# Stick-breaking attention: the softplus of the next step issued before the sum of the present one, half of its roundings on ScalarE

## The chip, the cores and the metric

The kernel runs on one core of one Trainium2 chip. The metric is the device time of one execution in microseconds, here the median of three runs. Engines are named TensorE (PE in the profile), VectorE (DVE), ScalarE (ACT), GpSimd (POOL) and SyncE (SP).

## What is computed

One layer of a decoder trunk: a modulated norm and input projection, a gated MLP beside stick-breaking attention, an output projection, then a mixture of 32 experts. The change touches the attention alone. With `z = q k / sqrt(128)` for 1024 tokens and 4 heads, it is

```python
log_fail = jnp.where(causal, jax.nn.log_sigmoid(-z), 0.0)
within = jnp.einsum('bhqni,ij->bhqnj', log_fail, after_in_block)
later = lax.cumsum(blk, axis=3, reverse=True) - blk
log_a = jax.nn.log_sigmoid(z) + (within + later[..., None])
a = jnp.where(causal, jnp.exp(log_a), 0.0)
outs.append(jnp.einsum('bhqk,bhkd->bhqd', a.astype(vt.dtype), vt[:, :, :kl]))
```

Here `-log_sigmoid(-z)` is the softplus of `z`, and `blk` is the sum of `log_fail` over a block of 128 keys.

## The kernel before, in words

The attention works on transposed scores: 128 keys on the partitions, up to 512 queries (half of the sequence) along the columns. A `Chain` is one head and one half of the queries; it goes through its blocks of keys `j` from the last to the first, 4 blocks in the first half and 8 in the second. A block on the diagonal needs only part of the columns: widths are 128, 256, 384, 512 in the first half and 128, 256, 384, then five times 512 in the second. Two chains (two heads, of even and odd number) run together as a pair; `seq` lists the 24 steps, each a block of both chains, twelve of them 512 wide and four of each other width.

In a step, for each chain: `z` (L655, with the mask L659 on the diagonal) makes the scores on TensorE; `e0`, `e1`, `e2` (L664, L669, L673) make log(1 + exp(-|z|)) on ScalarE; `sp` (L681) on VectorE makes the softplus max(z, 0) + e, `sh` (L682) rounds it to the matrix format, `sl` (L683) on GpSimd takes the remainder, so that the products with triangles of ones keep the precision; `ls` (L689) makes log_sigmoid(z); `tri` (L697 for `sh`, L698 for `sl`) adds the sum inside the block to `cum` in PSUM; `add` (L702) adds `cum` to `ls`; `comp` (L708, L709) completes `cum` to the sum over the whole block for the later steps, after `add` has read it; `exp` (L713) and the product with the values `av` (L719) finish it.

The order on every engine is written out by hand (`manual_schedule`): each engine's queue holds its instructions in the order of the program. In round `k` of the loop this is: tri(k), add(k), z(k+2), comp(k), av(k-1), sp(k+1) with its sh and sl, ls(k+1), e0(k+2), exp(k), e1(k+2), e2(k+2). When a pair is finished, six closing parts are put at the end of the next rounds: fin0 copies and squares the output (ScalarE, L724, L726), fin1 sums the squares on TensorE (L730) and takes a power on GpSimd (L128), fin2 spreads it by 16 products (L736), fin3 scales (VectorE, L740), fin4 rounds (ScalarE, L744), fin5 takes the remainder (VectorE, L748). The fourth pair is closed in the output projection that follows (L867).

Buffers that matter: four `z` in PSUM (two steps), two `sp`, four each of `e`, `sh` and `sl`, eight `ls`, two `cum`.

Of the kernel before, what the change touches and what calls it, by code (L numbers as in the profile page):

```python
# [13 lines left out]
AF = mybir.ActivationFunctionType  # L14
# [44 lines left out]
def body(ctx, tc, A, out):  # L59
    nc = tc.nc  # L60
    V, G, T, SC, SY = nc.vector, nc.gpsimd, nc.tensor, nc.scalar, nc.sync
# [364 lines left out]
    def at(s, fn):  # L426
        todo.setdefault(s, []).append(fn)
# [192 lines left out]
    def wo_load(i):  # L620
        if i < 16:
            cg, b = i // 4, (i + 2) % 4
            wo_raw[i] = wr.tile([P, 2, 512], F32, name="wo")
            SY.dma_start(wo_raw[i], A["w_out"][cg, b])
# [8 lines left out]
    def ya_load(t):  # L633
        y = op.tile([P, DG], F32, name="yld")
        SY.dma_start(y, y_d[t * P:(t + 1) * P, :])
        return y

    with ExitStack() as c3:
# [4 lines left out]
        class Chain:  # L643
# [31 lines left out]
            def sp(self, j):  # L675
                z, e = self.k[j]
                q0 = self.q0(j)
                sp = at_.tile([P, 512], F32, name="sp", bufs=2)[:, q0:]
                sh = at_.tile([P, 512], F32R, name="sh")[:, q0:]
                sl = at_.tile([P, 512], F32R, name="sl")[:, q0:]  # L680
                V.scalar_tensor_tensor(sp, z, 0.0, e, op0=ALU.max, op1=ALU.add)  # L681
                V.tensor_copy(sh, sp)  # L682
                G.tensor_tensor(sl, sp, sh.bitcast(F32), op=ALU.subtract)  # L683
                self.k[j] += [sh, sl]

# [66 lines left out]
        with tc.manual_schedule():  # L752
            seq = []
            for half in range(2):
                for hp2 in range(2):
                    ch = [Chain(half, 2 * hp2), Chain(half, 2 * hp2 + 1)]
                    seq += [(ch, j) for j in range((half + 1) * HT - 1, -1, -1)]
            n = len(seq)

            def each(i, f):  # L760
                if 0 <= i < n:
                    ch, j = seq[i]
                    for c in ch:
                        f(c, j)

            for i in range(2):
                wo_load(i)
            G.dma_start(wgr, A["w_gr"])
            yas = {t: ya_load(t) for t in range(2)}

            def scores(i):
                for f in (Chain.e0, Chain.e1, Chain.e2):
                    each(i, f)

            def first(i):
                return 0 <= i < n and seq[i][1] == seq[i][0][0].top

            each(0, Chain.z)
            each(1, Chain.z)
            scores(0)  # L780
            each(0, Chain.sp)
            each(0, Chain.ls)
            scores(1)
            for k in range(n + 1):
                each(k, Chain.tri)
                each(k, Chain.add)
                each(k + 2, Chain.z)
                each(k, Chain.comp)
                if 0 < k and seq[k - 1][1] == 0:
                    for i in range(6):  # L790
                        for c in seq[k - 1][0]:
                            at(k + (0, 1, 1, 1, 2, 3)[i], getattr(c, f"fin{i}"))
                if first(k - 2):
                    each(k - 2, Chain.av)
                if not first(k - 1):
                    each(k - 1, Chain.av)
                each(k + 1, Chain.sp)
                each(k + 1, Chain.ls)
                each(k + 2, Chain.e0)
                each(k, Chain.exp)  # L800
                each(k + 2, Chain.e1)
                each(k + 2, Chain.e2)
                for f in todo.pop(k, []) if k < n else ():
                    f()
            fins = [f for k in sorted(todo) for f in todo[k]]
            todo.clear()
# [710 lines left out]
```

## Time and profile before

| | us |
|---|---|
| median of 3 runs | 1617.72 (1617.65 to 1617.85) |
| profiled run, its own time | 1615.23 |
| its span, first to last instruction | 1613.4 |
| attention stage in the span | 535 to 663 |

The profile is of one execution. A row of the timeline gives the start in us from the start of the span, the duration, the engine, the source line, the operation with output and inputs, and in brackets how long the engine had been idle and who ended it. Instructions of one kind in a row are merged (x2: two, with one duration for both). The name `ls` stands for the tile that `ls`, `add` and `exp` share, `e` for that of `e0`, `e1`, `e2`. PEclk is the granted clock of TensorE, 1.00 for the upper of its two levels. The stage was cut out by the first `z` and the last `sl`.

### The profile page before, as it was taken

The page shows a single profiled execution, that of the slowest core. Times are in us where ns is not written, and L with a number is a line of the kernel's source. Part 1 is how long each engine was busy: PE and PEld are TensorE (multiplying, and loading weights), DVE is VectorE, ACT ScalarE, POOL GpSimd, SP SyncE. Part 2 cuts the span into 40 slices and gives each one's busy share as a digit, 9 for nine tenths or more (in the row PEclk, how much of TensorE's full clock was granted, in tenths as well). Part 3 has the DMA queues.
Part 4 walks back from the last instruction along what each step waited for, and adds up shares of the span by engine and source line. Part 5 has one row for each costly group of instructions (what it writes and reads, how often), then busy time and mean ns, then how long its engine had stood idle before and what let it go on. Part 6 is the DMA issues. An engine that isn't in the chain of part 4 may idle for free.

```text
span 1613.4 us, 21346 instructions
## 1 busy us (share of the span) xinstructions
PE 1518.8 (94%) x6818; PEld 1151.6 (71%) x6818; DVE 1221.2 (76%) x2220; ACT 945.1 (59%) x2014; POOL 315.2 (20%) x288
## 2 busy tenths in 40 slices
PE   4999998999999899899999869999989999999996
PEld 4788887888888665578878656666656666666664
DVE  5889675867787588668856768887868888888883
ACT  5442588755434667432223467777767777777771
POOL 2000132010011334320001322324221212211111
PEclk8899999999999999999999979999989999999998
DMA  9987478768776000468857568999999999999972
GB/s 378 351 315 242 155 260 297 258 238 310 279 258 228 1 1 1 154 211 299 291 187 289 200 209 318 354 369 346 387 341 365 360 361 370 366 362 356 358 299 33
DMA packets 94394, 433.94 MB, mean 269 GB/s; under 512 B 13073, under 2 KB 13185, under 8 KB 64193
## 3 DMA queue, kind: packets, MB, share of 16 engines
q1 hardware_dynamic: 82000, 377.54, 63.3%
q0 software_dynamic: 11984, 52.85, 11.2%
q10 hardware_dynamic: 288, 2.10, 0.3%
q8 instruction: 56, 0.92, 0.2%
q14 instruction: 66, 0.53, 0.1%
HBM read 399.89 MB, written 43.02 MB: 275 GB/s over the span
## 4 chain that ended last, share of the span: by engine, by line
PE 40%; DMA 34%; issue 13%; DVE 5%; ACT 4%; POOL 2%; POOLq 0%; another core or an unknown queue 0%; SPq 0%; DVEq 0%; ACTq 0%
DMA out<-y,idx 22%; PE acc L322 22%; PE acc L867 9%; DMA xg<-u_d,idx 7%; DMA out<-xi 2%; DMA wm<-in_w_mod 2%; PE lg L913 1%; PE yp L719 1%; POOL sl L683 1%; PE z L655 1%; DVE macc L182 1%; DVE sp L681 1%; ACT junk L347 1%; DVE sh L682 1%; PE tr L906 1%
## 5 line engine op out<-in xcount | busy, mean ns | idle before, releaser
L1282 DVE TENSOR_TENSOR wl<-wx,wh 128x1024 fp32r<-128x1024 f32 x256 | 309.5, 1219 | 13.5 <-ACT wh L1281 12.5
L1281 ACT ACTIVATE wh<-wx 128x1024 fp32r<-128x1024 f32 x256 | 273.4, 1070 | 49.0 <-PE gu L1291 34.8
L1314 PE MATMUL dn<-wx,actT 128*128 128x512 f32 x512 | 242.4, 597 | 6.1 <-DMA wx<-in_w_down 5.5
L1291 PE MATMUL gu<-wh,xh 128*128 128x512 f32 x512 | 239.7, 468 | 0.0
L182 DVE SCALAR_TENSOR_TENSOR macc<-wm,sc_c,macc 128x512 f32<-128x512 f32 x296 | 222.2, 751 | 11.5 <-DMA wm<-in_w_mod 3.4
L322 PE MATMUL acc<-wh,hh 128*128 128x512 f32 x640 | 209.8, 398 | 3.4 <-ACT hh L278 1.8
L322 PE MATMUL acc<-wl,hh 128*128 128x512 f32 x640 | 206.7, 393 | 2.9 <-DVE wl L307 2.7
L322 PE MATMUL acc<-wh,hl 128*128 128x512 f32 x640 | 206.6, 393 | 0.4 <-DVE hl L279 0.4
L1291 PE MATMUL gu<-wl,xh 128*128 128x512 f32 x512 | 203.1, 397 | 0.1
L1291 PE MATMUL gu<-wh,xl 128*128 128x512 f32 x512 | 201.9, 394 | 0.0
L1224 POOL DMA_INDIRECT out<-y,idx x52 | 94.9, 1825 | 459.2 <-DVE y L1315 453.1
L1315 DVE TENSOR_TENSOR y<-dn,gate 128x512 f32<-128x512 f32 x128 | 88.5, 692 | 112.0 <-PE dn L1314 101.6
L867 PE MATMUL acc<-wo,yh 128*128 128x512 f32 x512 | 169.3, 412 | 0.0
L1270 ACT ACTIVATE xh<-tp,b2c 128x128 fp32r<-128x128 f32 x512 | 146.8, 383 | 17.8 <-PE tp L1265 17.7
L1314 PEld LDWEIGHTS dn<-wx,actT 128*128 128x128 f32 x512 | 96.5, 189 | 82.6 <-issue 63.1
L1272 DVE SCALAR_TENSOR_TENSOR xl<-tp,b2c,xh 128x128 fp32r<-128x128 f32 x512 | 143.5, 343 | 3.9 <-ACT xh L1270 3.9
L322 PEld LDWEIGHTS acc<-wl,hh 128*128 128x128 f32 x640 | 120.7, 189 | 30.0 <-DVE wl L307 5.0
L322 PEld LDWEIGHTS acc<-wh,hl 128*128 128x128 f32 x640 | 121.2, 189 | 26.9 <-DVE hl L279 1.1
L322 PEld LDWEIGHTS acc<-wh,hh 128*128 128x128 f32 x640 | 119.6, 190 | 27.6 <-ACT hh L278 1.9
L307 DVE TENSOR_TENSOR wl<-w,wh 128x1024 fp32r<-128x1024 f32 x80 | 97.6, 1221 | 34.2 <-ACT wh L306 34.1
L306 ACT ACTIVATE wh<-w 128x1024 fp32r<-128x1024 f32 x80 | 83.0, 1053 | 63.1 <-PE acc L322 51.6
L1291 PEld LDWEIGHTS gu<-wl,xh 128*128 128x128 f32 x512 | 97.4, 190 | 30.2 <-issue 15.1
(246 smaller groups left out, 2326.7 us busy)
## 6 DMA issues: line engine op xcount, KB each, us to landing
wx<-in_w_gu SPq DMA_DIRECT2D x128, 1024.0 KB
wm<-in_w_mod SPq DMA_DIRECT2D x160, 512.0 KB
wx<-in_w_down SPq DMA_DIRECT2D x64, 1024.0 KB
w<-in_w_in SPq DMA_DIRECT2D x80, 512.0 KB
x<-in_w_mod SPq DMA_DIRECT2D x16, 1024.0 KB
wo<-in_w_out SPq DMA_DIRECT2D x16, 512.0 KB
xi<-in_x SPq DMA_DIRECT2D x24, 256.0 KB
out<-xi SPq DMA_DIRECT2D x24, 256.0 KB
```

The costliest lines, as they stand in the source:

```text
L182: V.scalar_tensor_tensor(self.acc, t[:, j, :], sc, self.acc, op0=ALU.mult, op1=ALU.add)
L307: V.tensor_tensor(wl, w, wh.bitcast(F32), op=ALU.subtract)
L322: T.matmul(accs[t], a, b, start=(first and j == 0 and n == 0), stop=(last and j == 1 and n == 2))
L867: T.matmul(acc, y[a][:, c, ts_], w[b][:, c % 2, :], start=(n_ == 0 and i == 0), stop=(n_ == 7 and i == 2))
L1224: return G.indirect_dma_start(out=out, out_offset=bass.IndirectOffsetOnAxis(ap=idx, axis=0), in_=y, in_offset=None, bounds_check=S - 1, oo ...
L1270: SC.activation(xh[:, j, :], self.p[:, j, :], AF.Identity, bias=b2c[:, b * 4 + j:b * 4 + j + 1])
L1272: V.scalar_tensor_tensor(xl[:, j, :], self.p[:, j, :], b2c[:, b * 4 + j:b * 4 + j + 1], xh[:, j, :].bitcast(F32), op0=ALU.add, op1=ALU.sub ...
L1281: SC.activation(self.wh[q], w, AF.Copy)
L1282: low = lambda: V.tensor_tensor(self.wl[q], w, self.wh[q].bitcast(F32), op=ALU.subtract)
L1291: T.matmul(self.gu, a[c // 4][:, c % 4, :], b[q][:, k, :], start=(c == 0 and i == 0), stop=(c == 15 and i == 2))
L1314: T.matmul(d, self.aT[:, f, :], self.wd[f][:, cs], start=(f == 0), stop=(f == 1))
L1315: V.tensor_tensor(self.y[:, cs], d, gate2[:, cs], op=ALU.mult)
```

## The change

It does two things. `sp` of the next step, with its rounding `sh` and its remainder `sl`, is issued right after the triangular product of the present step and ahead of `add`, where it stood behind `av`. And the rounding of every chain with an odd head number is done by ScalarE instead of VectorE. As the calls are ordered, that instruction stands in ScalarE's queue ahead of `e0`. Nothing else moves.

```diff
@@ -679,7 +679,10 @@
                 V.scalar_tensor_tensor(sp, z, 0.0, e, op0=ALU.max, op1=ALU.add)
-                V.tensor_copy(sh, sp)
+                if self.h % 2:
+                    SC.activation(sh, sp, AF.Copy)
+                else:
+                    V.tensor_copy(sh, sp)
                 G.tensor_tensor(sl, sp, sh.bitcast(F32), op=ALU.subtract)
                 self.k[j] += [sh, sl]
@@ -783,6 +786,7 @@
             for k in range(n + 1):
                 each(k, Chain.tri)
+                each(k + 1, Chain.sp)
                 each(k, Chain.add)
                 each(k + 2, Chain.z)
                 each(k, Chain.comp)
@@ -794,7 +798,6 @@
                 if not first(k - 1):
                     each(k - 1, Chain.av)
-                each(k + 1, Chain.sp)
                 each(k + 1, Chain.ls)
                 each(k + 2, Chain.e0)
                 each(k, Chain.exp)
```

## Rows read from the trace of the kernel before

**Rows 1.** Busy time by stretch (time, then engines with counts, PEclk, DMA share, GB/s)

```profile
535.00:663.00 128.00, 114.34 (x488) 77.55 (x488) 106.92 (x208) 91.52 (x210) 54.79 (x57) 0.97 0.05 17
586.30:589.80 3.50, 3.48 (x17) 3.48 (x18) 0.75 (x1) 0.85 (x2) 0.95 (x1) 0.56 0.02 5
```

**Rows 2.** Timeline of one wide step (start us, duration us, engine, line, what)

```profile
606.67 1.28 POOL L683 TENSOR_TENSOR sl<-sp,sh 128x512 fp32r<-128x512 f32 x1 [0.45 <-DVE sh L682]
...
608.54 0.69 DVE L702 TENSOR_TENSOR ls<-ls,cum 128x512 f32<-128x512 f32 x1 [0.24 <-PE cum L698]
...
609.14 0.68 DVE L681 SCALAR_TENSOR_TENSOR sp<-z,e 128x512 f32<-128x512 f32 x1
...
609.86 0.43 DVE L682 CAST sh<-sp 128x512 fp32r<-128x512 f32 x1
...
610.21 0.68 DVE L681 SCALAR_TENSOR_TENSOR sp<-z,e 128x512 f32<-128x512 f32 x1
...
610.92 1.11 DVE L682 CAST sh<-sp 128x512 fp32r<-128x512 f32 x1
...
611.79 1.14 ACT L669 ACTIVATE e<-e 128x512 f32<-128x512 f32 x2
...
612.20 1.29 POOL L683 TENSOR_TENSOR sl<-sp,sh 128x512 fp32r<-128x512 f32 x1 [0.45 <-DVE sh L682]
...
612.83 1.14 ACT L673 ACTIVATE e<-e 128x512 f32<-128x512 f32 x2
```

**Rows 3.** Groups by line, 535 to 665 us (busy, mean ns, then idle before)

```profile
L664 ACT ACTIVATE e<-z 128x512 f32<-128x512 f32 (+3 forms) x48 | 22.9, 489 | 32.8 <-PE z L659 16.5 <-PE z L655 16.2
```

**Rows 4.** The largest product group of the output projection, from the page

```profile
L867 PE MATMUL acc<-wo,yh 128*128 128x512 f32 x512 | 169.3, 412 | 0.0
```

**Rows 5.** Timeline of a step 256 columns wide

```profile
555.70 0.71 ACT L673 ACTIVATE e<-e 128x256 f32<-128x256 f32 x2
...
556.20 0.42 DVE L681 SCALAR_TENSOR_TENSOR sp<-z,e 128x256 f32<-128x256 f32 x1 [0.28 <-ACT e L673]
...
556.66 0.29 DVE L682 CAST sh<-sp 128x256 fp32r<-128x256 f32 x1
556.87 0.42 DVE L681 SCALAR_TENSOR_TENSOR sp<-z,e 128x256 f32<-128x256 f32 x1
```

**Rows 6.** Timeline at ScalarE's first and last work in the stage

```profile
535.77 0.25 ACT L664 ACTIVATE e<-z 128x128 f32<-128x128 f32 x1
...
663.71 0.67 DVE L702 TENSOR_TENSOR ls<-ls,cum 128x512 f32<-128x512 f32 x1
...
664.41 0.63 ACT L713 ACTIVATE ls<-ls 128x512 f32<-128x512 f32 x1 [3.95 <-DVE ls L702]
...
665.34 0.63 ACT L713 ACTIVATE ls<-ls 128x512 f32<-128x512 f32 x1 [0.30 <-DVE ls L702]
```

**Rows 7.** Timeline where a pair of chains is closed, twice

```profile
586.32 3.45 PE L736 MATMUL yp<-cst,rs 128*128 128x128 f32 x16 [0.91 <-POOL rs L128]
...
629.05 1.07 ACT L664 ACTIVATE e<-z 128x512 f32<-128x512 f32 x2
...
629.95 1.01 POOL L683 TENSOR_TENSOR sl<-sp,sh 128x384 fp32r<-128x384 f32 x1 [0.39 <-DVE sh L682]
...
630.91 1.99 POOL L128 TENSOR_TENSOR rs<-rs,mhalf 128x4 f32<-128x4 f32 x2
...
631.97 2.14 PE L736 MATMUL yp<-cst,rs 128*128 128x128 f32 x16 [0.92 <-POOL rs L128]
...
634.23 0.75 DVE L740 SCALAR_TENSOR_TENSOR u<-u,hcol,yp 128x512 f32<-128x512 f32 x1 [0.31 <-PE yp L736]
```

**Rows 8.** The chain that ended last, in time order (start us, us, what)

```profile
608.50 1.72 PE z L655 x4
610.22 0.23 PE cum L708
...
611.15 1.72 PE yp L719 x4
```

## The prediction

> **What bounds the kernel now.** I went from the stage to the engine and then to one step. The attention stage fills the stretch from 535 to 663 us of the profiled run; in it VectorE is busy for 106.92 of 128 us, TensorE for 114.34, ScalarE for 91.52, GpSimd for 54.79 [rows 1]. None is full, so a ring of waits must set the pace. The timeline of one step, in which both chains work on tiles of 512 columns, shows it [rows 2]. From one `sl` of the second chain (606.67) to the next (612.20) are 5.53 us, and this ring has no hole in it: `sl` on GpSimd and the triangular product behind it, 1.87 until the sum (`add`) of the second chain starts at 608.54; then on VectorE `add` 0.60 to the start of `sp`, 0.72 to `sh`, 0.35 to the second `sp`, 0.71 to the second `sh`, and 1.28 until the next `sl`. The second `sh` takes 1.11 where the first takes 0.43: it runs while GpSimd works on the first chain's `sl`. ScalarE, in the same step, waits: its `e0` lost 32.8 us in the stage to late scores `z` [rows 3], because `z` stands behind the triangular product, and this behind `sl`. After the stage TensorE goes straight into the output projection, whose products hardly wait (0.0 us before the largest group of them) [rows 4]; what the stage gains or loses reaches the end whole.
>
> **The change, part by part.** *The move* puts `sp`, `sh`, `sl` of the next step ahead of the sum of the present one. On VectorE the queue becomes sp, sh (chain 0), sp (chain 1), add, add, ls, ls; on GpSimd only the `sl` move, ahead of nothing but the powers of the closing steps (costed below), and what is moved issues no DMA, on no queue. It opens the ring above: `sp` no longer stands behind `add`, so the triangular product finds its `sl` ready. Its price is that the two sums, and so `exp` (ScalarE) and the complementary product (TensorE), now stand behind two `sp` that wait for `e2` of ScalarE.
>
> *The rounding on ScalarE* takes the 24 `sh` of the odd chains from VectorE, 1.11 us each in a wide step, and puts them on ScalarE **ahead of** `e0` of the step after. That instruction waits for `sp` of its chain, and behind it are queued e0, e0, exp, exp, e1, e1, e2, e2. The `sp` after it waits for that `e2`. So a new ring arises, ScalarE to VectorE and back, once a step.
>
> Its length in a wide step, counted from the start of `e2` of chain 0: two `e2` take 1.14 and stand 0.52 apart, as the start of `e1` (611.79) and of `e2` (612.83), two instructions each, tell: 1.04 for two. So the first ends at 0.62. From the end of an `e2` to `sp` it takes 0.10: 256 columns wide, a pair takes 0.71 and stands 0.31 apart, so the first ends at 556.10 and `sp` starts at 556.20 [rows 5]. Then 0.72 to `sh`, 0.35 to the second `sp`, 0.68 for it, and 0.03 from VectorE to ScalarE (the sum of 663.71 ends at 664.38, its `exp` starts at 664.41 [rows 6]). ScalarE can start `sh` at 2.50; its second `e2` ended at 1.14; it waits 1.36. From there to the next `e2`: `sh` 0.52, two `e0` 0.95 (1.07 for the pair, with an overlap of about 0.1 [rows 7]), exp 1.04, e1 1.04, together 3.55. The ring is **6.05 us against 5.53**.
>
> What is covered in it: the first sum starts at 2.39 and ends at 3.07, its `exp` is due at 3.97, 0.9 later. `sl` of chain 1 runs from about 3.27 to 4.55, and the triangular product comes round after 5.9. TensorE needs 1.72 for the scores, 1.72 for the value products and eight products with the triangles of 0.23, 5.3 of 6.05 us [rows 8]. VectorE needs 0.72 + 0.35 + 0.60 and four times 0.60, about 4.1. If any of this cover is gone, it adds to the 6.05, and never takes from it.
>
> Not every step is wide, so I sum the stage as a ledger of ScalarE, which works strictly in order: work and waits. **Before:** from its first `e0` (535.77) to the end of its last `exp` (665.34 + 0.63) 130.2 us [rows 6]; waits 32.8 [rows 3] and, for the last two `exp`, 3.95 and 0.30 [rows 6]; work 93.1. **After, work:** 24 `sh` more at the spacing of its instructions, 0.52 for 512 columns and 0.31 for 256 [rows 2, 5], by the line through them 0.41 and 0.20 for 384 and 128; of 24 steps twelve are 512 wide and four each of the others, so 12 x 0.52 + 4 x (0.41 + 0.31 + 0.20) = 9.9; minus about 1.0, because a wait exposes some 0.1 us of an instruction's end and there will be some ten waits fewer: 102.0. **After, waits:** before `sh` 1.36 in a wide step; 0.91 with 256 columns (555.70 to 556.20, 0.46, 0.21, 0.42 and 0.03 give 1.62, less the pair of 0.71); by the line 1.13 and 0.68 for 384 and 128. Where closing work of a finished pair stands in ScalarE's queue it fills these waits: fin4 (1.04) in two wide steps and one narrow one, the copy and the square of fin0 in three of 384. That leaves 7 x 1.36 + 2 x 0.32 + 4 x 0.91 + 3 x 0.68 + 1.13 = 17.0. Three wide `sh` come behind the closing of a pair. There VectorE holds `sp` behind fin3 (L740), which needs the powers on GpSimd and the products L736. From the start of the preceding `sh` (384 wide, behind the square): 0.5 for it, 0.17 to `sl` and 0.96 to its successor (629.95 to 630.91), 1.99 for two powers, 1.33 until fin3 of the second chain (634.23, counted from 632.90), 0.67 until the next instruction of VectorE, now `sp`, then 0.72, 0.35, 0.68, 0.03 as above [rows 2, 7]: 7.4. ScalarE has 4.1 of work in that time (0.41, 0.95, 0.62, 1.04, 1.04), so it waits some 3.2, three times, 9.6. Waits for `z` remain where a narrow `sp` lets ScalarE run ahead of TensorE, after the last wide step of each pair; the trace of before can't show them. They lie between nothing and what `e0` loses now per step (32.8 over 24, 1.4), twice over for three such places, 8; I take 4. The last `exp` waits for `sh` 0.62, `sl` 0.17 + 1.28, product and sum about 1.2: 3.3. Together 33.9. **The sum:** 102.0 + 33.9 = 135.9 against 130.2, **5.7 us longer**.
>
> **TensorE's clock** I leave as it is. It fell in the stage: from 586.3 to 589.8 the mean granted clock was 0.56, partly at the lower of its two levels, 1.2 instead of 2.4 GHz [rows 1], after TensorE had waited 0.91 us for the powers [rows 7]. The sixteen products L736 took 3.45 there and 2.14 at 631.97 [rows 7]; I take the difference, 1.3 us, for one fall. That wait stays in the new order; whether it meets a fall more or less often, no row tells: minus 2 to plus 4 for the range.
>
> **The rivals.** *Faster.* The second `sh` leaves the ring in which it took 1.11, and ScalarE's answer comes early enough. Then TensorE's 5.3 bounds a wide step: twelve times 0.22, 2.6 us, and up to as much again in the narrow steps: 3 to 5 less, **1613 to 1615**. It needs ScalarE's wait before `sh` to be under 1.36 - 0.52 = 0.84. For it: VectorE is the busiest engine apart from TensorE [rows 1], and in wide steps alone it loses 12 x 1.11 = 13 us of casts. Against it: each link of the 2.50 has its row, and they are in series. The Trainium skill, "SBUF — State Buffer", section "Who interferes with whom", says that a cast of VectorE in a mode with two ports and a GpSimd instruction exclude each other, the later one waiting for the whole of the first; the trace agrees (1.11 against 0.43), and by that rule alone the change would give back 0.68 for each wide step, 8 us in twelve.
>
> *No change.* The waits for `z` don't appear (4 less), and at the closings TensorE and VectorE come round earlier than I chain them, with some 0.7 less each: 1617 to 1620.
>
> *Slower than I say.* TensorE's idle time in a step grows from 0.2 to 0.7, and the clock falls in three or four more stretches, at 1.3 each: 4 to 5 on top, about **1628**. The Trainium skill, "TensorE: Matmul & The Clock Gate", section "HAM oscillation — how this bites in real kernels", tells of kernels in which waits between bursts of products keep taking the clock down.
>
> *The move does not do what it says*, because the sums hold up `exp` on ScalarE: it decides once they come over 0.9 us later than I have them. It would add to 6.05 and lies in the upper part of the range.
>
> **How the numbers follow.** The profiled run took 1615.23, the median of three runs is 1617.72, 2.5 more; I add 5.7 to the median: **1623.4**. My forecast (1621 to 1626) gets 0.52, slower still 0.15, no change 0.18, faster 0.15. A measurement of this kernel can tell about 0.2% from no change, 3.2 us. So faster 0.15, same 0.18, slower 0.67. The range leaves out most of faster and the far end of slower: 1616.0 to 1629.5.
>
> **What would show it.** Right: wide steps about 6.05 apart; ScalarE waiting some 26 us before `sh`, named after `sp`, and its waits for `z` down from 32.8 to a few us; the remaining casts of VectorE at 0.43; VectorE idle before `sp`, for `e2`; GpSimd hardly waited for by the triangular product. Wrong: wide steps at 5.3 with ScalarE waiting under 0.84 before `sh`; or `exp` waiting for the sums throughout; or a stage of the same length with its loss in the closings only.

## The result, and the profile after

The changed kernel took 1628.22 us (median of 4 runs, 1626.99 to 1631.31) against 1617.78 for the kernel before: 10.4 us longer, a ratio of 1.0068 with a 95% interval of 1.0054 to 1.0082. The direction was right and the time lies inside the range; the forecast of 1623.4 has about half of the loss. Of all single runs of this study one, of the kernel e4 below, took 1734.0 us at a mean granted clock of 0.84 (the others 0.97 to 0.98) and is left out of its ratio.

The profiled run of the changed kernel took 1629.25, 14.0 more than that of before. The loss splits into three stretches, by ScalarE's first `e0` and the end of its last `exp`:

| | before | after | difference |
|---|---|---|---|
| up to the first `e0` of the stage | 535.77 | 537.52 | +1.75 |
| the stage | 130.20 | 141.35 | **+11.15** |
| from its end to the end of the run | 949.3 | 950.4 | +1.1 |

The first row is not the change's: in the profiled runs of all kernels below this start lies anywhere from 533.8 to 539.7. The stage holds the loss. Its two ends are rows of ScalarE's timeline after (start, duration, engine, line, what):

```profile
537.52 0.25 ACT L664 ACTIVATE e<-z 128x128 f32<-128x128 f32 x1
...
677.64 1.23 ACT L716 ACTIVATE ls<-ls 128x512 f32<-128x512 f32 x2 [4.56 <-DVE ls L705]
```

The projection behind it hands the loss on whole, as before (its largest group of products, from the page after, beside [rows 4]):

```profile
L870 PE MATMUL acc<-wo,yh 128*128 128x512 f32 x512 | 170.5, 414 | 0.0
```

The groups by line of the changed kernel, 535 to 677 us (busy, mean ns, then idle before), stand beside [rows 3]. After, `sp` is L681, `sh` is L683 on ScalarE and L685 on VectorE, `sl` L686, the triangular products L700 and L701, `add` L705, the complementary products L711 and L712, `exp` L716, the value products L722, the closing's products with the powers L739. First two groups of the kernel before (535 to 665 us), then those of the change:

```profile
L681 DVE SCALAR_TENSOR_TENSOR sp<-z,e 128x512 f32<-128x512 f32 (+3 forms) x48 | 26.4, 551 | 2.8 <-ACT e L673 2.7
...
L698 PE MATMUL cum<-sl,tri_r 128*128 128x512 f32 (+3 forms) x48 | 19.1, 401 | 10.7 <-POOL sl L683 10.7
```

```profile
L681 DVE SCALAR_TENSOR_TENSOR sp<-z,e 128x512 f32<-128x512 f32 (+3 forms) x48 | 26.6, 554 | 34.4 <-ACT e L673 17.4 <-issue 16.9
...
L664 ACT ACTIVATE e<-z 128x512 f32<-128x512 f32 (+3 forms) x48 | 21.0, 480 | 5.7 <-PE z L659 5.7
...
L701 PE MATMUL cum<-sl,tri_r 128*128 128x512 f32 (+3 forms) x48 | 17.6, 374 | 0.3
L711 PE MATMUL cum<-sh,comp_r 128*128 128x512 f32 (+3 forms) x40 | 17.1, 438 | 17.2 <-DVE ls L705 17.1
...
L685 DVE CAST sh<-sp 128x512 fp32r<-128x512 f32 (+3 forms) x24 | 8.6, 360 | 1.9
```

The wait for `z` has gone from 32.8 to 5.7 us, and TensorE no longer waits for GpSimd ahead of the second triangular product (0.3 us at L701, where it was 10.7 at L698). In their place VectorE stands idle for 34.4 us before `sp` (2.8 before), and TensorE for 17.2 before the complementary product, for the sums (0.2 before). The waits of ScalarE, from the view of waits (engine and line, waited for: total, times, longest), are:

```profile
ACT sh L683 <- DVE sp L681: 30.3, 20, 4.4
ACT e L664 <- PE z L659: 5.7, 7, 3.2
ACT ls L716 <- DVE ls L705: 4.6, 1, 4.6
```

One wide step after, from the timeline, beside [rows 2]:

```profile
614.70 1.14 ACT L673 ACTIVATE e<-e 128x512 f32<-128x512 f32 x2
...
615.43 0.69 DVE L681 SCALAR_TENSOR_TENSOR sp<-z,e 128x512 f32<-128x512 f32 x1 [2.00 <-ACT e L673]
...
616.22 0.43 DVE L685 CAST sh<-sp 128x512 fp32r<-128x512 f32 x1
...
616.56 0.68 DVE L681 SCALAR_TENSOR_TENSOR sp<-z,e 128x512 f32<-128x512 f32 x1
616.82 2.53 POOL L686 TENSOR_TENSOR sl<-sp,sh 128x512 fp32r<-128x512 f32 x2 [3.70 <-DVE sh L685]
617.16 1.27 DVE L705 TENSOR_TENSOR ls<-ls,cum 128x512 f32<-128x512 f32 x2
617.34 0.63 ACT L683 ACTIVATE sh<-sp 128x512 fp32r<-128x512 f32 x1 [1.50 <-DVE sp L681]
617.88 1.07 ACT L664 ACTIVATE e<-z 128x512 f32<-128x512 f32 x2
...
618.83 1.15 ACT L716 ACTIVATE ls<-ls 128x512 f32<-128x512 f32 x2
...
620.91 1.14 ACT L673 ACTIVATE e<-e 128x512 f32<-128x512 f32 x2
```

From one `e2` to the next are 6.21 us, and the path between them is the ring that the prediction wrote down: `e2`, `sp`, cast, `sp`, then `sh` on ScalarE, and from there ScalarE's own queue. ScalarE waits 1.50 before `sh`.

The 5.53 us that the prediction read off one step are what most wide steps took before, but not all. From the first `sp` of a wide step to that of the next wide one there are eight distances in the second half of the queries. Before, five took 5.5 us, two 6.61 and one 6.23, together 47.1; after, six take 6.21 and two 5.92, together 49.1. In a step of 6.61 VectorE takes the remainders of a finished pair (fin5) ahead of the sums:

```profile
601.01 1.49 DVE L748 TENSOR_TENSOR yl<-u,yh 128x512 fp32r<-128x512 f32 x2
```

After, the same two instructions (L751, at 607.13) find VectorE idle, and their step takes 6.21. So these wide steps lose 2.0 us together.

The granted clock of TensorE, by stretches (time, engines, PEclk; beside [rows 1]: the whole stage, then two places where it fell):

```profile
537.50:676.50 139.00, 118.70 (x483) 79.72 (x484) 85.89 (x184) 99.40 (x233) 56.40 (x58) 0.94 0.05 16
...
552.60:559.40 6.80, 5.92 (x17) 5.18 (x18) 3.90 (x9) 2.89 (x10) 3.36 (x4) 0.51 0.00 1
573.00:576.60 3.60, 3.60 (x19) 3.60 (x17) 2.08 (x3) 0.62 (x2) 0.02 (x1) 0.53 0.00 0
```

The stage as a whole was at 0.97 before and is at 0.94 after; 0.51 is almost wholly the lower of the two levels, 1.2 GHz. Before, the clock fell twice in the stage (566.2 to 569.7 and 586.7 to 590.2, 0.51 in both), after, four times (also 641.2 to 644.7 and 671.9 to 675.4). The first fall, 6.8 us long, has no counterpart before. What TensorE did ahead of it, in the timeline:

```profile
549.82 0.30 PE L659 MATMUL z<-negm_r,ident_r 128*128 128x128 f32 x1
...
553.48 0.69 PE L711 MATMUL cum<-sh,comp_r 128*128 128x384 f32 x1 [3.35 <-DVE ls L705]
...
554.93 2.76 PE L722 MATMUL yp<-ls,x 128*128 128x128 f32 x8
```

TensorE sits idle for 3.35 us, because the scores of that step are 128 columns wide and soon done, while the next products wait for sums that now stand behind two `sp` of 512 columns. This is the step in which the two widths part the most. It took 7.37 us.

### The profile page after: what moved, and what is told of

The parts are those of the page before. It is cut to its first block, busy times and chain, and to the rows that moved or that the text cites. A ratio compares the mean times of both kernels' runs of the same rounds, so it can differ in the third digit from the quotient of the medians.

```text
span 1627.3 us, 21294 instructions
## 1 busy us (share of the span) xinstructions
PE 1524.8 (94%) x6818; PEld 1155.6 (71%) x6818; DVE 1199.4 (74%) x2196; ACT 953.8 (59%) x2038; POOL 315.6 (19%) x288
## 4 chain that ended last, share of the span: by engine, by line
DMA 28%; PE 17%; issue 12%; ACT 5%; DVE 3%; POOL 1%; POOLq 0%; another core or an unknown queue 0%; DVEq 0%; ACTq 0%
DMA out<-y,idx 20%; PE acc L870 9%; DMA xg<-u_d,idx 5%; DMA out<-xi 2%; PE gu L1294 2%; PE lg L916 1%; PE dn L1317 1%; DVE sp L681 1%; PE tr L909 1%; ACT e L669 1%; ACT e L664 1%; ACT ls L716 1%; PE yp L739 1%; PE yp L722 0%; PE tp L1268 0%
## 5 line engine op out<-in xcount | busy, mean ns | idle before, releaser
L1284 ACT ACTIVATE wh<-wx 128x1024 fp32r<-128x1024 f32 x256 | 273.8, 1072 | 47.1 <-PE gu L1294 35.6
```

Source lines behind the costliest of these rows:

```text
L1284: SC.activation(self.wh[q], w, AF.Copy)
```

## The experiments

All times are medians of 4 to 10 runs; each ratio is against the kernel before on the same chip, where that took 1617.0 to 1617.6 (single runs 1611 to 1622). "Stage" is the stretch above in the profiled run (130.2 before, 141.35 after). "Wide step" gives the distance that occurs most often, or the range, and in brackets the mean of the eight distances named above (before 5.53, mean 5.89; after 6.21, mean 6.14).

| kernel | us | ratio (95%) | stage | wide step |
|---|---|---|---|---|
| the change, again (e5) | 1627.82 | 1.0078 (1.0060 to 1.0097) | 141.89 | 6.21 (6.14) |
| move alone (e1) | 1634.64 | 1.0119 (1.0095 to 1.0142) | 151.35 | 6.46 (6.35) |
| rounding alone (e2) | 1628.61 | 1.0082 (1.0058 to 1.0105) | 138.60 | 6.14 (6.09) |
| ScalarE's work without the wait (e3) | 1616.10 | 0.9999 (0.9983 to 1.0015) | 129.23 | 5.52 (5.88) |
| change, TensorE filled (e6) | 1626.14 | 1.0064 (1.0047 to 1.0080) | 135.21 | 6.21 (6.14) |
| the same again (e9) | 1623.81 | 1.0048 (1.0031 to 1.0064) | 138.35 | 6.21 (6.14) |
| move, rounding behind `e0` (e7) | 1625.36 | 1.0057 (1.0035 to 1.0079) | 140.43 | 5.3 to 6.3 (5.79) |
| no move, rounding behind `e0` (e8) | 1619.02 | 1.0022 (1.0010 to 1.0034) | 131.96 | 5.1 to 6.4 (5.57) |
| sum, `sp`, sum, `sp` (e4) | 1611.08 | 0.9967 (0.9954 to 0.9981) | 121.63 | 5.35, 4.7 to 6.0 (5.35) |
| `sp`, sum, sum, `sp` (e10) | 1615.04 | 0.9981 (0.9966 to 0.9997) | 127.13 | 4.7 and 6.1 in turn (5.44) |
| e4, value products earlier (e11) | 1608.39 | 0.9939 (0.9914 to 0.9963) | 121.55 | 4.6 to 6.0 (5.31) |

**Each part alone.** The move without the rounding:

```diff
                 each(k, Chain.tri)
+                each(k + 1, Chain.sp)
                 each(k, Chain.add)
...
-                each(k + 1, Chain.sp)
                 each(k + 1, Chain.ls)
```

> The move alone, all roundings on VectorE as before. Ring theory (what sets the pace is the chain of waits through the queue orders): the sums, and with them exp, now stand behind both sp and both casts of the next step, which wait for e2, and the second cast is still stretched beside GpSimd; counted from an e2 of the first chain, exp can start at about 4.2 and the next e2 at about 6.4, so a wide step takes 6.3 to 6.5 us, ScalarE waits for the sums (10 us and more before exp in the stage), and the kernel is 9 to 15 us slower than before, more than the whole change. Rival (the rounding on ScalarE alone costs the time, the move is harmless or opens the old ring): within 2 us of before, or faster.

It took 17 us more than before, beyond what was expected. Groups by line (here `sh` is L682, `add` L702, `exp` L713), and below them one wide step:

```profile
L682 DVE CAST sh<-sp 128x512 fp32r<-128x512 f32 (+3 forms) x48 | 28.3, 590 | 3.9
...
L713 ACT ACTIVATE ls<-ls 128x512 f32<-128x512 f32 (+3 forms) x48 | 23.4, 521 | 19.7 <-DVE ls L702 19.5
```

```profile
616.47 1.27 POOL L683 TENSOR_TENSOR sl<-sp,sh 128x512 fp32r<-128x512 f32 x1 [3.46 <-DVE sh L682]
...
617.01 1.02 DVE L682 CAST sh<-sp 128x512 fp32r<-128x512 f32 x1
...
617.95 1.27 DVE L702 TENSOR_TENSOR ls<-ls,cum 128x512 f32<-128x512 f32 x2
...
618.65 1.23 ACT L713 ACTIVATE ls<-ls 128x512 f32<-128x512 f32 x2 [0.53 <-DVE ls L702]
```

The stretched cast stays (1.02 beside GpSimd's subtract), now ahead of the sums, and `exp` waits for them, 19.7 us in the stage. Here the rival "the move does not do what it says" is the case. TensorE's clock was at its lower level for 27 us of this stage.

The rounding without the move:

```diff
-                V.tensor_copy(sh, sp)
+                if self.h % 2:
+                    SC.activation(sh, sp, AF.Copy)
+                else:
+                    V.tensor_copy(sh, sp)
```

> The rounding of odd chains on ScalarE alone, sp behind the sums as before. Ring theory: the same ring e2 - sp - sh - sp - rounding on ScalarE - e0 - exp - e1 - e2 is there, since the rounding stands ahead of e0; wide steps 6.1 to 6.2 us, ScalarE waiting some 30 us before the rounding, 4 to 9 us slower than before. Rival (the move is what costs, because the sums hold up exp and the complementary products): within 2 us of before.

It took 11 us more than before, again beyond what was expected. From its groups by line:

```profile
L716 ACT ACTIVATE ls<-ls 128x512 f32<-128x512 f32 (+3 forms) x48 | 22.5, 522 | 1.0 <-DVE ls L705 1.0
...
L664 ACT ACTIVATE e<-z 128x512 f32<-128x512 f32 (+3 forms) x48 | 20.6, 478 | 0.5 <-PE z L659 0.5
```

`e0` and `exp` hardly wait any more; what is left of ScalarE's idle time, 36.9 us, stands before `sh`. The ring through ScalarE is 6.14 a wide step with the sums ahead of `sp`, and the three closings take 10.7 each, with the clock low in them. So each part alone costs as much as the change or more, and the two losses do not add: taking the cast off VectorE gives the move back some 7 us of its 17, and beside the rounding on ScalarE the move brings nothing that can be told from noise (ratios 1.0082 without it, 1.0068 and 1.0078 with it).

**Is it ScalarE's extra work, or the wait?** The kernel before, with 24 copies of `e` of the same sizes at the place of the rounding, into a tile that nothing reads; they wait for nothing new:

```diff
                 V.tensor_copy(sh, sp)
+                if self.h % 2:
+                    SC.activation(at_.tile([P, 512], F32R, name="xx", bufs=1)[:, q0:], e, AF.Copy)
```

> Before, with 24 more copies on ScalarE at the place where the change puts the rounding and of the same size, but of a tile that ScalarE made itself and that nobody reads; casts stay on VectorE. Ring theory: no new wait, and ScalarE has 38 us of waits to take it, so 0 to 3 us slower, wide steps 5.5 us. Rival (ScalarE's additional work of 10 to 12 us is what costs): 7 to 11 us slower.

```profile
L664 ACT ACTIVATE e<-z 128x512 f32<-128x512 f32 (+3 forms) x48 | 22.6, 486 | 20.9 <-PE z L659 11.8 <-PE z L655 9.1
...
L684 ACT ACTIVATE xx<-e 128x512 fp32r<-128x512 f32 (+3 forms) x24 | 12.5, 520 | 0.6
```

12.5 us of work more on ScalarE, no time more: the wait for `z` shrinks from 32.8 to 20.9, by the work that fills it. What costs is not the length of the rounding but its waiting for VectorE at the head of ScalarE's queue; e3 leaves out both the wait and the use of the result, and the place in the queue is varied by itself in e7 and e8 below.

**The clock.** To see the change without falls, products whose result is never read fill TensorE's long waits: four calls of 512 columns (eight products in the trace) ahead of the complementary product of the one step above, and one call of 256 columns for each chain in each of the three closings.

```diff
+            def fill(self, n, w, src):
+                for _ in range(n):
+                    T.matmul(self.yp[:, 0:w], ident, src[:, 0:w], start=True, stop=True, skip_group_check=True)
...
+                if k == 2:
+                    for c in seq[0][0]:
+                        c.yp = py.tile([P, 512], F32, name="yp")
+                        c.fill(2, 512, qT[:, c.h, 0:512])
...
+                        if i == 2 and k < n:
+                            for c in seq[k - 1][0]:
+                                at(k + 1, lambda c=c: c.fill(1, 256, c.sq))
```

> The change, with products that do nothing useful where TensorE waits and its clock fell in the first profile: four of 512 columns in the second round (behind its scores, ahead of the complementary products, which wait 3.35 us there for the sum) and one of 256 columns for each chain in three closings, ahead of the products L739. Nobody reads what they write. If the falls of the clock are what my prediction lacked: no fall near the fourth step and at the closings, that step down from 7.4 to about 5, the closings at 8 to 8.5, the stage 3 to 5 us shorter than the change's own. Rival (the waits alone make the time, the clock follows them at no cost): the stage as long as the change's or up to 3 us longer, by the filling products themselves.

> The change as it is, once more, as the yardstick of the next three on the same chip. Ring theory: wide steps 6.2 us, ScalarE waiting 30 us before the rounding, 8 to 13 us slower than before; the falls of TensorE's clock need not lie in the same places as in the first profile.

The granted clock in the stage of the filled kernel, then its waits on ScalarE, then the step that took 7.37 us in the change (its L739 of this form is the filling):

```profile
538.80:674.00 135.20, 119.42 (x509) 77.67 (x510) 87.07 (x186) 100.60 (x236) 56.47 (x58) 1.00 0.05 16
```

```profile
ACT sh L683 <- DVE sp L681: 28.3, 20, 3.3
ACT e L664 <- PE z L659: 3.1, 7, 1.1
ACT ls L716 <- DVE ls L705: 3.1, 1, 3.1
```

```profile
551.22 3.65 PE L739 MATMUL yp<-xk,cst 128*128 128x512 f32 x8
...
554.74 0.44 PE L711 MATMUL cum<-sh,comp_r 128*128 128x384 f32 x1
...
555.65 1.47 PE L722 MATMUL yp<-ls,x 128*128 128x128 f32 x8
```

The clock stayed at 1.00 throughout, the value products took 1.47 instead of 2.76, and the stage took 135.21 us instead of 141.35. The steps that differ are the four where the change had lost its clock: that step 4.75 for 7.37; the first and third closing (from the first `sp` of the 384-wide step to that of the next) 8.09 and 8.05 for 9.00 and 9.24; the last stretch, from the first `sp` of the last step to the end of the last `exp`, 7.96 for 9.46. Together 2.62 + 0.91 + 1.19 + 1.50 = 6.22, against a difference of 6.14; in the second closing, where the change had not lost its clock, the filling costs 0.11, and every other step is the same to 0.01.

The repeat of the change (e5) tells the same, with five falls, in part at other places. The step after the 3.35 us wait came out at 6.02 there, since its fall was half as long:

```profile
549.30:552.80 3.50, 3.02 (x10) 2.93 (x11) 2.81 (x7) 2.62 (x10) 2.21 (x3) 0.51 0.01 2
```

Against the filled kernel e5 loses 1.28 in that step, 1.64 in the like step at the start of the third pair, 1.09 and 1.18 in two closings and 1.50 in the last stretch: 6.69, which is the whole difference of the stages (141.89 and 135.20).

The median fell by only 1.7 us against the change on the same chip. The profiled run of the filled kernel entered its stage at 538.78, 5 us later than that of the repeated change (533.83), which hides its gain in these two runs (1625.09 and 1626.09); for the medians this is not shown. The second trial:

> The change with the filling products of e6 once more, to see whether the stage of 135.2 us and the missing falls of the clock repeat, and where the time goes that the stage won (its start lay 5 us later than in the change's profile). If the falls are the missing term: no fall between 540 and 670 us, stage 135 to 136 us, median 2 to 6 us under the change's 1627.8. Rival (chance of one execution): falls as in the change, stage 140 us or more.

The median was 6.2 us above the kernel before (ratio 1.0048); the profiled stage 138.35, with two falls left, in one closing (9.81) and in the last stretch (9.46). Less what these two took beyond the 8.16 and 7.96 of e6, it is 135.2 again. So the filling takes falls away (none and two in the profiled stages, four and five without it), not every fall in every execution.

**Where the rounding stands in ScalarE's queue.** Rounding behind `e0` instead of ahead of it, with the move and without (the odd chains' `sh` and `sl` leave `Chain.sp` and are issued by a function of their own):

```diff
+            def rnd(self, j):
+                if self.h % 2:
+                    sh, sl = self.k[j][-2:]
+                    SC.activation(sh, self.sp_, AF.Copy)
+                    G.tensor_tensor(sl, self.sp_, sh.bitcast(F32), op=ALU.subtract)
...
                 each(k + 2, Chain.e0)
+                each(k + 1, Chain.rnd)
                 each(k, Chain.exp)
```

> The change, but the rounding on ScalarE stands behind e0 of the step after instead of ahead of it; sp ahead of the sums as in the change. Ring theory: e0 fills most of the wait before the rounding (1.50 down to about 0.5 in a wide step); but sl of chain 1, and the triangular product behind it, come later, and the sums still stand behind sp: wide steps 5.7 to 6.0 us, 1 to 4 us faster than the change. Rival (ScalarE's queue order does not matter, only that VectorE and ScalarE alternate): as the change.

> Only the rounding of odd chains on ScalarE, behind e0 of the step after; sp behind the sums as before. Ring theory: the ring through ScalarE has slack, the cast of 1.11 is gone from VectorE; wide steps 5.3 to 5.5 us, within 2 us of before or up to 4 us faster, and 8 us or more faster than the rounding ahead of e0. Rival (rounding on ScalarE costs by itself): 4 us or more slower than before.

With the move, ScalarE's wait before `sh` falls from 30.3 to 4.9 us, and the wait of `e0` for `z` comes back, 28.4: the ring closes elsewhere, and 8 us of loss stay. Without the move the wide steps are shorter than before (5.57 in the mean for 5.89; most take 5.1 to 5.4, those with fin5 6.3), as was hoped, but the closings take 10.0 to 11.1 where they took 8.4 to 9.7, and the sum is 2 us longer than before. The timeline of such a closing (here `sh` is L692, `sl` L693, the products with the powers L745):

```profile
630.99 1.06 ACT L664 ACTIVATE e<-z 128x512 f32<-128x512 f32 x2
...
631.94 0.52 ACT L692 ACTIVATE sh<-sp 128x384 fp32r<-128x384 f32 x1
...
632.54 1.00 POOL L693 TENSOR_TENSOR sl<-sp,sh 128x384 fp32r<-128x384 f32 x1 [1.35 <-ACT sh L692]
...
633.50 1.98 POOL L128 TENSOR_TENSOR rs<-rs,mhalf 128x4 f32<-128x4 f32 x2
...
634.56 2.77 PE L745 MATMUL yp<-cst,rs 128*128 128x128 f32 x16 [1.87 <-POOL rs L128]
```

The rounding stands on ScalarE behind the closing's own copies and squares and behind `e0`; `sl` on GpSimd comes after it, and the powers after `sl`. Counted from `e0`, the powers start 2.51 us later, where they started 1.86 later before (630.91 less 629.05 in [rows 7]), and TensorE waits 1.87 for them instead of 0.92.

**Orders on VectorE alone.** If two `sp` ahead of two sums hold up the sums, and two sums ahead of two `sp` hold up `sl`, then one of each in turn should do better than both, with every cast on VectorE (`one(k, c, f)` runs `f` for chain c of step k alone; `sp` is gone from its place behind the value products):

```diff
-                each(k, Chain.add)
+                for c in range(2):
+                    one(k, c, Chain.add)
+                    one(k + 1, c, Chain.sp)
```

> No rounding on ScalarE; on VectorE the order is sum of chain 0, sp and cast of chain 0, sum of chain 1, sp and cast of chain 1. Ring theory: between the two casts now lie a sum and an sp (about 1.3 us), so the second cast hardly meets GpSimd's 1.28 us of the first and falls from 1.11 to about 0.5; sp of chain 0 waits for one sum only; a wide step is then bounded by TensorE, 5.3 us against 5.53, and the kernel is 2 to 6 us faster. Rival (VectorE's order does not matter because the clock of TensorE and the closing steps set the stage): within 2 us of before.

It beats the kernel before by 0.33% (1611.08), at the upper end of what was expected, with a stage of 121.63 and no fall of the clock in it. One of its wide steps in the timeline (lines as in the kernel before):

```profile
608.45 0.69 DVE L702 TENSOR_TENSOR ls<-ls,cum 128x512 f32<-128x512 f32 x1 [0.66 <-PE cum L698]
...
609.06 0.68 DVE L681 SCALAR_TENSOR_TENSOR sp<-z,e 128x512 f32<-128x512 f32 x1
...
609.77 0.43 DVE L682 CAST sh<-sp 128x512 fp32r<-128x512 f32 x1
...
610.12 0.68 DVE L702 TENSOR_TENSOR ls<-ls,cum 128x512 f32<-128x512 f32 x1
610.37 1.29 POOL L683 TENSOR_TENSOR sl<-sp,sh 128x512 fp32r<-128x512 f32 x1 [2.32 <-DVE sh L682]
610.72 0.68 DVE L681 SCALAR_TENSOR_TENSOR sp<-z,e 128x512 f32<-128x512 f32 x1
...
611.43 0.51 DVE L682 CAST sh<-sp 128x512 fp32r<-128x512 f32 x1
```

The second cast takes 0.51, since the sum between the two `sp` lets GpSimd's subtract nearly end before it. The stretch of the cast goes away by order alone, and ScalarE needs no work for it. What it is worth by itself is not shown, for the order also changes what stands behind what: a wide step is 0.54 shorter in the mean. The other mixed order, both sums between the two `sp`:

```diff
+                one(k + 1, 0, Chain.sp)
                 each(k, Chain.add)
+                one(k + 1, 1, Chain.sp)
```

> All roundings on VectorE; its order is sp and cast of chain 0, both sums, sp and cast of chain 1. Ring theory: the casts lie 1.9 us apart, so none is stretched; sp of chain 0 goes ahead of the sums, as in the change, but exp stands behind one sp and cast only: wide steps at TensorE's 5.3 us, stage 121 to 124 us, 4 to 9 us faster than before, like e4. Rival (any sp ahead of the sums holds up exp as in the move alone): 4 us or more slower than before.

It gained less than expected, 2.6 us: its wide casts are not stretched at all (0.43 in the mean), but wide steps are 4.7 and 6.1 in turn, the closings take 9.3 to 9.9 (7.9 in e4), and the clock fell in three places (565.3, 585.7, 630.1). Last, the interleaved order with the value products ahead of the complementary ones in TensorE's queue, so that something is left to do while the sums come:

```diff
+                each(k, Chain.comp)
```

(behind the value products of the earlier step, and gone from its place ahead of them).

> e4 with the value products ahead of the complementary ones on TensorE, so that these no longer hold up a ready value product while they wait for the sum. Ring theory: wide steps were bounded by TensorE at 5.35 us already; the narrow ones gain a few tenths each: 0 to 3 us faster than e4, 5 to 10 us faster than before. Rival: the complementary products now come late for the next triangular product, and it is 1 to 3 us slower than e4.

1608.39, 0.9939 (0.9914 to 0.9963), the fastest kernel of this study, some 9 us under the kernel before. TensorE's wait ahead of the complementary product falls from 5.1 us in e4 to 0.3 in the stage. That it is faster than e4 is not shown: the two intervals overlap, the two ran on different chips, and the profiled stages are alike (121.63 and 121.55, the latter with two falls of the clock).

## Why the prediction was right, and where half of the loss was missing

**Right: the ring.** Wide steps of 6.05 were forecast and are 6.21. Of the 0.16, 0.14 is in ScalarE's wait (1.50 for 1.36): 0.07 because the first `sp` of a step, now behind an idle VectorE, stands 0.79 ahead of the cast (615.43 to 616.22) instead of the 0.72 of [rows 2], and 0.07 because ScalarE's `sh` starts 0.10 after the second `sp` ends instead of the 0.03 taken from [rows 6]. The waits for `z` went to 5.7, the remaining casts take 0.43, and VectorE is idle for `e2`: the marks named for "right" are all there. That the wait and not the work is the price was argued in the prediction and is shown by e3.

**The wide steps are the smaller part.** The prediction set 6.05 against one step of 5.53, but the wide steps before took 5.89 in the mean. Without falls of the clock (the filled kernel; before less the 2.0 worked out below) the stage loses 7.0 us, to rounding: 2.0 in the eight wide steps, 4.1 in the steps with a narrow tile, 1.7 in the last stretch, and the closings give 0.9 back. The ledger did not suffer by this, for it counts ScalarE's work and waits over all widths.

**Right: the ledger, at an unfallen clock.** Its terms for ScalarE, beside the filled kernel (no fall) and the change:

| | forecast | filled | change |
|---|---|---|---|
| work | 102.0 | 100.7 | 100.8 |
| waits before `sh` | 26.6 | 28.3 | 30.3 |
| waits for `z` | 4 | 3.1 | 5.7 |
| the last `exp` | 3.3 | 3.1 | 4.6 |
| stage | 135.9 | 135.2 | 141.4 |

Work came out 1.3 lower, the waits before `sh` 1.7 higher; the sum is off by 0.7, in part because these two misses cancel. The 3.2 us chained for a closing are the filled kernel's longest wait before `sh`, 3.3.

**Wrong: "TensorE's clock I leave as it is".** This is the step that failed. The change's own falls account for the 6.1 us between its two columns, all of it in waits of ScalarE. The 130.2 of the kernel before already held two falls, one of them in [rows 7]: its closings took 9.06, 9.69 and 8.39, some 2.0 more than three of 8.39. So the sum did not leave the clock as it was: it set an after without falls against a before with 2.0 us of them. At an unfallen clock the change costs 135.2 - 128.2 = 7.0; the falls add 6.1 - 2.0 = 4.1; together the 11.1 of the stage. The rival "Slower than I say", with 4 to 5 us of clock on top and 1628, is what happened; it had 0.15. Its mechanism was right, and its size nearly so: it counted three or four more falls at 1.3; the first profile has two more, one of them twice as long and dear (2.6), the repeat three more at 1.1 to 1.6. The prediction bounded the clock by minus 2 to plus 4 without a row behind either number, and 4.1 is at that bound: that the measured time lies inside the range owes something to luck. The Trainium skill, "TensorE: Matmul & The Clock Gate", section "HAM oscillation — how this bites in real kernels", which it put beside that rival, tells of waits between bursts of products that keep taking the clock down. The trace agrees, with the granted clock at 0.51 in 552.6 to 559.4, after a wait of 3.35 us.

The runs without a profile bear this out in part. Every run has its mean granted clock on record, over its whole length: 0.9748 in the mean for the kernel before on the chip of e5 and e6, 0.9722 for the change and 0.9742 for the filled kernel; 0.9735 and 0.9746 for before and e9 on theirs. So the change loses clock without a profile too: by an estimate from these means (0.0026 of 1624 us, lost at half the clock) it spends some 8 us more at the lower level than the kernel before, and the filling gives most of that back. In time the filling gives back less than in the profiled stage: 1.7 us of the median on the same chip, and 4.0 in the second trial, on another.

What could have been read in advance: a step with 128-wide scores beside a 512-wide `sp` leaves TensorE without work. The prediction weighed TensorE's idle time in a wide step alone (0.2 to 0.7), and the gap arose where the widths differ.

**The other rivals.** *Faster* needed a wait before `sh` under 0.84; it is 1.50. The stretch of 0.68 in the second cast can indeed be won back, and e4 wins most of it by order alone (0.51 for 1.11); in the change the cast is gone from VectorE, and the longer ring uses up what that gives. *No change* needed the waits for `z` to be absent and cheaper closings; neither came. *The move does not do what it says* is true of the move alone (e1: `exp` waits 19.7 us for sums) and not of the change: there the rounding on ScalarE keeps the sums early, and `exp` waits for them only at the end.

**Open.** How many falls an execution has differs between runs of the same kernel (e6 and e9), and why is not settled; so is the difference between the filled kernel's stage, 5.0 us over that of before, and its medians, 9.1 and 6.2 over. More falls in the executions without a profile are hardly the reason: the mean clock of the filled kernel's runs is that of the kernel before, to 0.001.

## What to carry to other kernels

An instruction moved to an engine with idle time is paid for by what it waits for and what is queued behind it in order, and not by its length: 24 copies, 12.5 us of extra work, cost nothing here, and 24 roundings of the same length that wait on VectorE cost eleven when they came alone. Before moving work off an engine because one instruction on it is stretched by another, try the order on that engine: one sum between two pairs of `sp` and cast took most of the stretch away, and that order gained 6 us. Read more than one step before taking its length for all: the closing's work made two of eight wide steps 1.1 longer. And where an edit lets TensorE run out of work, look for its waits step by step, at steps of unequal width too, and put the clock there into the sum as a term, on both sides.

## What the runs showed of the hardware that was not expected

A fall of TensorE's clock to its lower level costs 0.7 to 1.7 us in a closing and 1.5 in the last stretch. After one and the same wait of 3.35 us it cost 2.6 in one execution, where 6.8 us ran at 0.51, and 1.3 in another, where 3.5 us did. Useless products of 3.65 us, placed in that wait, took the whole cost away in both filled executions; the steps without a fall repeat to 0.01 us from one profiled execution of the change to the other.

Two casts to fp32r that met a GpSimd subtract ended equally long after it, although one started 0.73 us ahead of its end and the other 0.23: in e1 the subtract ends at 617.74 and the cast at 618.03; in e4 the subtract ends at 611.66 and the cast at 611.94. Some 0.28 us after the end in both, with cast durations of 1.02 and 0.51, against 0.43 alone. The cast of 1.11 in [rows 2] ends at 612.03, the subtract beside it at 611.75: 0.28 again.
